# A streaming encoder layer: TensorE, VectorE, ScalarE and GpSimd keep the order of the calls in the first part

## The chip, the cores and the metric

The kernel runs on one core of a Trainium2 chip. The metric is device time in microseconds from launch to end; the median of three runs is given. A core has TensorE (matmuls, PE in the profile, its weight loads PEld), VectorE (DVE), ScalarE (ACT), GpSimd (POOL) and SyncE (SP, which here only issues DMAs). Each engine works through a queue of its own from the front; engines wait for one another, and for DMAs, through semaphores.

## The reference

One layer of a streaming encoder, in float32, over a prompt of 2048 tokens and a sample of 64 tokens, with a model width of 1024. Cut to what matters:

```python
h = rms_norm(x, norm1_g) * (1 + sc1) + sh1            # sc, sh, gt: silu(c) @ w_ada + b_ada, in six parts
glu_a, glu_b, q, k, v, g_conv, g_attn = split(h @ w_in)   # 512 columns each, the gates 1024
u = glu_a * sigmoid(glu_b)
conv_out = silu(layer_norm(causal_depthwise_conv(u, 31 taps) + b_dw)) @ w_conv_out
q, k = rms_norm(q per head), rms_norm(k per head)      # 8 heads of 64
o = band_attention(q, k, v, rel_bias)                  # chunks of 64: own chunk and the 8 before it
x = x + gt1 * ((sigmoid(g_conv) * conv_out + sigmoid(g_attn) * (o @ w_attn_out)) @ w_o)
gate, up = split((rms_norm(x, norm2_g) * (1 + sc2) + sh2) @ w_ffn_in)   # 2816 each
x = x + gt2 * ((silu(gate) * up) @ w_ffn_out)
```

Outputs are the two results, the last convolution inputs, and the keys and values to be cached.

## The kernel before

**Products.** Operands are split into a high and a low part of a shorter format (`hi` by a ScalarE copy, `lo` by a VectorE or GpSimd subtraction), and each product is three matmuls: high by high, high by low, low by high (`mm3`). Weights come by DMA into `wst`, are split into `whi` and `wlo`, stored as split, and loaded again when a later block needs them.

**First part** (it ends at `p1.close()`, line 1689). The 2112 tokens are worked in four blocks (`PBLOCKS`: 576, 512, 512, 512). A block goes through q, a piece of GLU, k, a piece of GLU, v, two pieces of GLU, and the 16 column tiles of the two gates (`ORDER`). Beside these products run, as Python generators:

- the row norm of the next block (`norm_tile`, line 1172): load of `x_t`, squares on ScalarE, the root `r` on GpSimd, the scaled rows on VectorE, transposes `pt` on TensorE, and `h`, `hh`, `hl`;
- the convolution (`convolve`): 31 taps as multiply-adds `y` on VectorE, and its norm (`conv_norm`, line 1289), with sums on GpSimd and a column sum `pm` on TensorE;
- attention (`attend`, line 1495), 8 heads for each block, and 8 for the sample beside block 0: score matmuls `sc`, a maximum and a sum `sm`, exponentials `pr`, transposes `ptp`, the product `po`. The q and k of a head are read back by DMA into `q2` and `kk` (`load_qk`, line 1406); each of the two tiles has one buffer, which in block 0 is divided between a prompt head and a sample head.

**What sets the order.** A planner (`Stream`) adds up a cost for each call and engine, its estimate of the time by which that engine is through. A generator yields the time at which it may go on, and its lane takes it up again when TensorE's estimate has passed that time. For attention this reads:

```python
    def fetch(i):
        if i < len(order) and i not in loaded:
            ...
            loaded[i] = stream.load["pe"] + DMA_LAG
```

`DMA_LAG` is 4000 ns. `attend(i)` calls `fetch(i + 1)` when it has given out its last scores (line 1530), and the next head yields `loaded[i]` (line 1503) before its first score matmul. Two heads may be under way at once.

The sequence of calls that comes of this isn't yet the sequence on the engines. The framework's scheduler takes the calls with their dependencies and sorts each engine's instructions by its own estimate of when they are ready; a call that isn't ready by that estimate lets later ones pass. Edges such as `tc.issue_after(...)`, which the kernel sets in a few places (the first block, the taps behind the last softmax), hold some instructions back.

The relative bias is prepared once, between q and k of block 0 (`bias_rows`, line 1015): a load of `rv` on ScalarE's DMA queue, three VectorE operations that make `rr`, and a store of `rr` to `rb_d` on ScalarE's queue.

**Second part.** Merge, output projection and the feed-forward network, by other pools and lanes. It isn't touched.

Of the kernel before, what the change touches and what calls it, by code (L numbers as in the profile page):

```python
# [589 lines left out]
def weight_order():  # L590
    yield from (("qkv", 0, k) for k in range(4))
    for b, stage in ORDER:
        if stage == "g":
            for g in range(0, 16, 2):
                yield from (("in", 2560 + g * P, h) for h in range(2))
        elif stage in ("q", "k", "v"):
            if b or stage != "q":
                yield from (("qkv", "qkv".index(stage), k) for k in range(4))
        else:
            yield from (("in", CONV + stage * P), ("in", stage * P))  # L600
    for s in range(len(CBLOCKS)):
        for _ in range(2):
            yield from (("ca", c) for c in range(KT))
            yield from (("wo", k) for k in range(KT))
        yield from (("fi", f * P) for f in range(EARLY))
        for f in range(0, NF, 2):
            ops = up_operands(f) + up_operands(f + 1)
            for j in range(0, len(ops), 2):
                yield ("up", *ops[j : j + 2])
                if f >= 2 and seven(s, f - 2):  # L610
                    yield from (("dn", s, f - 2, *DOWN_OPERANDS[i]) for i in {0: (0,), 2: (1, 2), 4: (3,)}.get(j, ()))
                elif j == 0 and f >= 2 and f - 2 not in last_rows(s):
                    yield from (("fo", f - 2), ("fo", f - 1))
        yield from (("fo", f) for f in last_rows(s))
# [3 lines left out]
def streaming_layer(ctx: ExitStack, tc: tile.TileContext, I, O):  # L618
# [159 lines left out]
    def temp(name, shape=(P, 512)):  # L778
        return wk.tile(list(shape), F32, tag="t", name=name, bufs=NT)
# [116 lines left out]
    def mod_steps():  # L896
        for c6, half in MOD_HALVES:
            pa = ps_g.tile([P, 512], F32, tag="gp", name="pa")
            mod_sums(pa[:, : 2 * P], [("mod", c6, half, i) for i in range(4)])
            R = mod_rows(pa[:, : 2 * P])  # L900
            stream.at(
                stream.when("dve") + TURN_LAG, lambda pa=pa, R=R, c6=c6, half=half: mod_columns(pa[:, 2 * P :], R, c6, 4 * half, 2)
            )
            yield
        stream.flush()
        pt = ps_g.tile([P, 512], F32, tag="gp", name="pt")
        pe.transpose(pt[:32, :P], gates_c.rearrange("p c s k -> p (c s k)"), ident)
        row = temp("row")
        dve.tensor_copy(row[:32, :P], pt[:32, :P])
        nc.sync.dma_start(gt_d.rearrange("c s (k n) -> (c s k) n", n=P), row[:32, :P])  # L910
        yield
# [121 lines left out]
    def store_kq(src, n, dst, col, g=None):  # L1033

        pt = ps_g.tile([P, 4, P], F32, tag="gp", name="pt")
        for hp in range(4):
            pe.transpose(pt[:, hp, :n], src[:n, hp * P : (hp + 1) * P], ident[:n, :n])
        stream.after("act", "pe")
        hi, lo = parts(shape=(P, 4, P))
        if g is None:  # L1040
            split(hi[:, :, :n], lo[:, :, :n], pt[:, :, :n])
        else:
            act.activation(hi[:, :, :n], pt[:, :, :n], AF.Copy, scale=g)
            stream.after("dve", "act")
            dve.scalar_tensor_tensor(lo[:, :, :n], pt[:, :, :n], g, hi[:, :, :n].bitcast(F32), ALU.mult, ALU.subtract)

        def store():
            for j, t in enumerate((hi, lo)):
                nc.sync.dma_start(dst[j, :, :, col : col + n].rearrange("h p t -> p h t"), t[:, :, :n].bitcast(F32))

        stream.at(stream.when("act", "dve"), store)

    def store_v(src, n, row):
        vst = wa.tile([P, 4, 4, HD], F32R, tag="x", name="vst", bufs=3)
        s = src[:n].rearrange("p (a c d) -> p a c d", a=4, c=2)
        stream.after("act", "pe")
        act.activation(vst[:n, :, 0:4:3], s, AF.Copy)
        stream.after("dve", "act")
        dve.tensor_tensor(vst[:n, :, 1:3], s, vst[:n, :, 0:4:3].bitcast(F32), ALU.subtract)
        stream.at(stream.when("act", "dve"), lambda: nc.sync.dma_start(  # L1060
            v_d[row : row + n].rearrange("t h d -> t (h d)"), vst[:n].rearrange("p a c d -> p (a c d)").bitcast(F32)
        ))
# [37 lines left out]
    def cached_kv():  # L1100
        rows_ = [(src, j) for j in range(CACHE // P) for src in (ck, cv)]
        ts = []
        for i, (src, j) in enumerate(rows_):
            for src_, j_ in rows_[len(ts) : i + 2]:
                t = temp("cache")
                nc.sync.dma_start(t, src_[j_ * P : (j_ + 1) * P])
                ts.append((t, stream.load["pe"] + CACHE_LAG))
            t, landed = ts[i]
            yield landed
            if src is ck:  # L1110
                store_kq(t, P, k_d, j * P)
            else:
                store_v(t, P, j * P)
            yield
# [506 lines left out]
    xs = first_rows()  # L1621
    W = Weights((nc.sync, act, dve, gps), wpool, dram, stream, list(weight_order()), source, 3, 5, lambda key: key[0] in KEPT)
    first_block(xs)
    norm_lane.add(cached_kv())
    mods = mod_steps()
    norms = {}
# [59 lines left out]
    tail.drain()  # L1686
    stream.flush()
    side.close()
    p1.close()


# [663 lines left out]
```

## Time and profile before

| | |
|---|---|
| runs | 2960.14 us median of 3 (2956.6 to 2961.68) |
| the profiled execution | 2958.2 us |
| its span, first to last instruction | 2956.1 us |
| granted TensorE clock, mean | 0.996 |
| HBM | 476.53 MB read, 148.54 MB written |

Times within the trace are microseconds from the start of the span. In rows of a timeline the columns are start, duration, engine, line, operation, what it writes and reads, shape and count; in brackets stands the idle time of the engine before it and what ended that. Nearly all operations are recorded under line 102, where a helper passes the calls on, so they are told apart by their tiles. A row of the busy times by stage gives the stretch, its length, busy time and number of instructions of each engine, the granted TensorE clock as a share, the share of the DMA engines that was busy, and GB/s.

### The profile page before, as it was taken

What the parts mean: (1) busy time and instruction counts of PE and PEld (TensorE: products, weight loads), DVE (VectorE), ACT (ScalarE), POOL (GpSimd) and SP (SyncE); (2) the same over time, 40 slices, a digit from 0 to 9 for tenths busy, and PEclk for the clock granted to TensorE, in tenths of its full rate; (3) what the DMA queues carried; (4) which work ended last, traced back from release to release, by engine and by line L of the source; (5) the groups of instructions that cost most, each with busy time, mean ns of one, the idle gap of its engine ahead of it and who ended that gap; (6) DMA issues with size and microseconds to landing.
All of it is one profiled execution on the core that took longest, in us unless ns stands there. A gap on an engine that the chain in (4) does not pass through costs nothing.

```text
span 2956.1 us, 44848 instructions
## 1 busy us (share of the span) xinstructions
PE 2895.5 (98%) x16193; PEld 2587.1 (88%) x16193; DVE 2041.9 (69%) x3648; ACT 1363.3 (46%) x2453; POOL 1166.4 (39%) x753
## 2 busy tenths in 40 slices
PE   8999899999999999999999999999999999999999
PEld 5899777787888788888999998999999999999998
DVE  5897687668857885577777746676666547566666
ACT  3345633661465257464433345444444345444442
POOL 1101310111011103454566452366667742465767
PEclk9999999999999999999999999999999999999999
DMA  9988889988987889985444776332333965333333
GB/s 320 320 291 293 285 277 299 286 260 275 303 277 221 277 248 286 280 293 172 150 152 146 261 256 228 99 118 93 114 122 104 332 223 185 97 96 111 115 107 126
DMA packets 467066, 628.04 MB, mean 212 GB/s; under 512 B 36196, under 2 KB 314584, under 8 KB 466845
## 3 DMA queue, kind: packets, MB, share of 16 engines
q1 hardware_dynamic: 452944, 606.11, 63.1%
q10 hardware_dynamic: 13901, 19.08, 1.8%
q8 instruction: 127, 2.08, 0.3%
q14 instruction: 94, 0.77, 0.1%
HBM read 476.53 MB, written 148.54 MB: 211 GB/s over the span
## 4 chain that ended last, share of the span: by engine, by line
PE 48%; DVE 2%; ACT 1%; issue 1%; DMA 0%; POOL 0%; ACTq 0%; DVEq 0%
PE ps L102 29%; PE pd L102 14%; PE pw L102 5%; DVE wlo L102 1%; DVE pw L102 0%; ACT whi L102 0%; DVE ps L102 0%; DVE t L102 0%; DMA tg<-g_d 0%; DVE sums L102 0%; PE pt L102 0%; DVE acc L102 0%; ACT xn L102 0%; DVE hid L102 0%; ACT hid L102 0%
## 5 line engine op out<-in xcount | busy, mean ns | idle before, releaser
L102 PE MATMUL ps<-t,whi 128*128 128x384 f32 (+1 forms) x2112 | 501.7, 322 | 3.0 <-DVE u L102 0.9
L102 POOL TENSOR_TENSOR wlo<-wst,whi 128x1024 fp32r<-128x1024 f32 (+1 forms) x159 | 363.7, 2298 | 243.3 <-ACT whi L102 231.0
L102 ACT ACTIVATE whi<-wst 128x1024 fp32r<-128x1024 f32 (+1 forms) x265 | 258.3, 979 | 321.8 <-PE ps L102 135.0
L102 PE MATMUL ps<-b,whi 128*128 128x384 f32 (+1 forms) x1584 | 381.6, 326 | 6.4 <-ACT early L102 2.7
L102 PEld LDWEIGHTS ps<-t,whi 128*128 128x128 f32 x2112 | 367.7, 188 | 10.2 <-ACT u L102 3.3
L102 DVE SCALAR_TENSOR_TENSOR y<-u,wd,y 128x512 f32<-128x512 f32 (+1 forms) x480 | 369.3, 773 | 6.3
L102 PE MATMUL ps<-hh,whi 128*128 128x512 f32 (+2 forms) x992 | 361.6, 365 | 0.0
L102 DVE TENSOR_TENSOR acc<-acc,pd 128x512 f32<-128x512 f32 x482 | 322.2, 684 | 48.5 <-PE pd L102 46.0
L102 PE MATMUL ps<-hl,whi 128*128 128x512 f32 (+2 forms) x992 | 345.6, 348 | 0.0
L102 PE MATMUL ps<-hh,wlo 128*128 128x512 f32 (+2 forms) x992 | 345.1, 348 | 0.0
L102 PE MATMUL ps<-t,wlo 128*128 128x384 f32 (+1 forms) x1056 | 338.2, 321 | 0.0
L102 PE MATMUL pd<-whi,hid 128*128 128x512 f32 x912 | 297.2, 391 | 0.3 <-DVE hid L102 0.3
L102 PEld LDWEIGHTS ps<-b,whi 128*128 128x128 f32 x1584 | 278.0, 189 | 14.5 <-ACT early L102 4.1
L102 POOL TENSOR_TENSOR r<-t,mhalf 128x1 f32<-128x1 f32 (+2 forms) x68 | 84.1, 1244 | 444.5 <-DVE t L102 434.2
L102 PE MATMUL ps<-b,wlo 128*128 128x384 f32 (+1 forms) x792 | 256.8, 324 | 0.0
L102 ACT ACTIVATE pr<-pr,sm 128x640 f32<-128x640 f32 (+3 forms) x272 | 200.2, 747 | 111.8 <-DVE sm L102 109.2
L102 PEld LDWEIGHTS ps<-hh,wlo 128*128 128x128 f32 x992 | 186.7, 188 | 21.7
L102 PEld LDWEIGHTS ps<-hh,whi 128*128 128x128 f32 x992 | 187.1, 189 | 18.6 <-issue 1.9
L102 DVE TENSOR_TENSOR wlo<-wst,whi 128x1024 fp32r<-128x1024 f32 (+1 forms) x106 | 135.1, 1277 | 98.7 <-ACT whi L102 97.2
L102 PEld LDWEIGHTS pd<-whi,hid 128*128 128x128 f32 x912 | 171.1, 188 | 36.2 <-ACT hid L102 0.7
L102 PEld LDWEIGHTS ps<-hl,whi 128*128 128x128 f32 x992 | 187.5, 189 | 15.5 <-issue 1.4
L102 PEld LDWEIGHTS ps<-t,wlo 128*128 128x128 f32 x1056 | 198.1, 188 | 0.8
(233 smaller groups left out, 6297.4 us busy)
## 6 DMA issues: line engine op xcount, KB each, us to landing
whi<-w_din_h SPq DMA_DIRECT2D x72, 512.0 KB, 6.7
wlo<-w_din_l SPq DMA_DIRECT2D x72, 512.0 KB, 7.5
wst<-sum_d SPq DMA_DIRECT2D x131, 256.0 KB, 2.9
wfo<-in_w_ffn_out SPq DMA_DIRECT2D x64, 512.0 KB, 4.1
wmod<-in_w_ada SPq DMA_DIRECT2D x46, 512.0 KB, 9.0
sum_d<-ws SPq DMA_DIRECT2D x88, 256.0 KB, 2.0
wst<-in_w_ffn_in SPq DMA_DIRECT2D x85, 256.0 KB, 3.3
wst<-in_w_in SPq DMA_DIRECT2D x40, 512.0 KB, 7.6
```

Of the source, the lines that this page charges most:

```text
L102: self.last = f(*args, **kw)
```

## The change

A region is opened after the first block has been set up and closed at the end of the first part. In it, the four named engines get their instructions in the order in which the kernel makes the calls. SyncE isn't among them. No call is added, removed or moved.

```diff
     first_block(xs)
+    ordered = ExitStack()
+    ordered.enter_context(tc.manual_schedule(engines={mybir.EngineType.PE, mybir.EngineType.DVE, mybir.EngineType.Activation, mybir.EngineType.Pool}))
     norm_lane.add(cached_kv())
     mods = mod_steps()
     ...
     side.close()
+    ordered.close()
     p1.close()
```

## The prediction

> **What bounds the kernel now.** I read the page first (busy times), then the busy times by stage, then the waits of TensorE in the first part, then single stretches of the timeline.
>
> ```profile
> span 2956.1 us, 44848 instructions
> PE 2895.5 (98%) x16193; PEld 2587.1 (88%) x16193; DVE 2041.9 (69%) x3648; ACT 1363.3 (46%) x2453; POOL 1166.4 (39%) x753
> ```
> ```profile
> core 0: us, PE busy (x) PEld busy (x) DVE busy (x) ACT busy (x) POOL busy (x), PEclk, DMA share, GB/s
> 62.00:296.00 234.00, 228.42 (x1518) 209.38 (x1517) 192.39 (x339) 108.43 (x221) 39.29 (x37) 1.00 0.88 297
> 296.00:444.00 148.00, 137.94 (x757) 111.97 (x757) 112.99 (x260) 74.01 (x166) 34.16 (x24) 0.97 0.86 282
> 444.00:592.00 148.00, 143.65 (x754) 116.42 (x753) 102.07 (x192) 68.98 (x121) 13.73 (x15) 0.99 0.93 293
> 592.00:1182.00 590.00, 581.68 (x3173) 491.44 (x3173) 438.53 (x843) 298.78 (x543) 74.45 (x62) 1.00 0.83 268
> ```
> ```profile
> engine line waited for: us in total, times, longest us
> PE pt L102 <- DVE x_t L102: 8.2, 3, 5.6
> PE sc L102 <- DVE sm L102: 5.7, 5, 2.4
> PE pm L102 <- POOL s L102: 5.6, 4, 1.9
> PE ps L102 <- DMA whi<-w_dqkv_h: 2.6, 1, 2.6
> PE pt L102 <- DVE kn L102: 1.4, 2, 1.3
> ...
> PE sc L102 <- DMA kk<-k_d: 0.3, 1, 0.3
> ```
>
> TensorE is the bound: 98% over the span. The four stages are what the new region covers after its start; the orders of the two programs differ up to about 1181 us of this trace and are the same behind it. In them TensorE is busy 1091.7 of 1120 us, so all idle time that a better order could win there is 28.3 us. The third fence tells whom TensorE waited for in this stretch. The three largest rows are 19.5 us; waits for the q and k loads of attention are 0.3 us in all. VectorE is at 82, 76, 69 and 74%: second, with room.
>
> **What the order does.** The change adds and removes no computation. In the before kernel a scheduler sorts what the kernel gives out; in the new one each of the four engines keeps the sequence of the calls. Set against each other, 1,480 TensorE instructions have another place, by 7 places on average, and 1,334 on VectorE, 699 on ScalarE, 125 on GpSimd. Since an engine works its queue from the front, an instruction that is moved ahead of its operand holds up all that stands behind it. I therefore looked, on TensorE, for instructions that stand much earlier than before, and asked when the trace shows their operands. SP is not in the region; its loads stay tied to the same events.
>
> **Step A: the first score matmuls of a head.** Tiles `q2` and `kk` have one buffer, so the four loads of the next head can be issued only once the last score matmul of this head is through:
>
> ```profile
> 579.10 0.86 PE L102 MATMUL sc<-kk,q 128*128 128x320 f32 x4
> 583.42 0.39 PE L102 MATMUL ps<-hl,whi 128*128 128x512 f32 x1
> 583.64 0.39 PE L102 MATMUL ps<-hh,wlo 128*128 128x512 f32 x1
> 590.04 0.82 PE L102 MATMUL sc<-kk,q 128*128 128x320 f32 x4 [0.32 <-DMA kk<-k_d]
> ```
> ```profile
> 579.99 0.61 SPq L1418 DMA_DIRECT2D q<-q_d  x1
> 580.65 0.75 SPq L1419 DMA_DIRECT2D kk<-k_d  x1
> 581.45 0.60 SPq L1418 DMA_DIRECT2D q<-q_d  x1
> 582.09 0.79 SPq L1419 DMA_DIRECT2D kk<-k_d  x1
> ```
> ```profile
> kk<-k_d SPq DMA_DIRECT2D x48, 256.0 KB, 6.1
> kk<-k_d SPq DMA_DIRECT2D x16, 80.0 KB, 3.2
> ```
>
> The last score matmul ends at 579.10 + 0.86 = 579.96, and the loads go out from 579.99 to 582.09. The next head's first score matmul came at 590.04 and still waited 0.32 us: the data took 10.1 us from the last score matmul. By the median the last load lands 582.09 - 579.96 + 6.1 = 8.2 us after it. In the scheduler's order 42 to 72 instructions fill such a pause. The kernel's own order gives out the next scores as soon as its estimate says that the load has landed (`DMA_LAG`, 4 us). In blocks 1 to 3, at 11 of the 24 heads, only about seven products of three matmuls lie between: 8 times exactly 21 matmuls, once 21 and a transpose, twice as much work in smaller pieces with 8 transposes. A 128x512 matmul starts 583.64 - 583.42 = 0.22 to 0.23 us after the one before it, so the cover is 21 x 0.227 = 4.8 us. The shortest pauses before, some 42 instructions or 8 us, showed no wait, so the data is usually there within 8; I take 7.3. The wait is 7.3 - 4.8 = 2.5 us, x 11 = **+27 us**. Low end: last issue 2.1 + the shortest median 3.2 = 5.3, so 0.5 x 11 = 6. High end, with 10.1: 58. What hid the load was the transposes and products that now stand behind the scores; they are still done afterwards, so nothing pays for the wait.
>
> **Step B: a block's first head.** In blocks 0 and 1 its first score matmul is moved ahead by 85 and 54 instructions. For block 1:
>
> ```profile
> 457.30 0.44 SPq L1419 DMA_DIRECT2D kk<-k_d  x1
> 468.67 0.74 PE L102 MATMUL sc<-kk,q 128*128 128x320 f32 x4
> ```
>
> Fifty-four places at 0.227 are 12.3 us: TensorE would be there at 456.4, when the last load goes out at 457.30 and lands 6.1 later, at 463.4. That is 7 us if SP stays where it is, 0 if the load moves up as well. For two heads 0 to 14; I take +10, nearer the high end, since the loads stand behind weight loads on SP and the DMA engines are 0.86 to 0.93 busy there.
>
> **Step C: transposes and sums that now stand in front.** In block 1 the first column sum of the convolution's norm stands 25 instructions earlier, yet its operand ended the wait in this row:
>
> ```profile
> 540.39 1.13 PE L102 MATMUL pm<-s,ones 128*128 128x512 f32 x2 [1.27 <-POOL s L102]
> ```
>
> Moved up by 25 x 0.227 = 5.7 us it would wait 1.27 + 5.7 = 7 us. Three groups of `ptp` transposes, moved up likewise, are 3 to 5 us each. Up to 20 in all; most goes away because TensorE comes later there anyway (A and B): **+6**.
>
> **Step D: the bias rows.** The load of `rv` and the store of `rb_d` now stand one behind the other on ScalarE, and VectorE's three `rr` operations between them are late:
>
> ```profile
> L102 DVE TENSOR_SCALAR rr<-rv x1: 281/281/281, 60.0 to 60.0; 8x256 f32<-8x256 f32 x1
> L1018 ACTq DMA_DIRECT2D rv<-in_rel_bias x1: 302/302/302, 17.8 to 17.8; - x1
> ```
> ```profile
> 119.93 1.06 ACT L102 ACTIVATE whi<-wst 128x1024 fp32r<-128x1024 f32 x1 [3.68 <-DMA wst<-in_w_in]
> ```
>
> Before, the load had 42 us. Now ScalarE issues it at about 113 and stands at the store until VectorE has worked down to `rr`, by its queue some 10 us later. Queued behind: a part of the keys, two tanh, and the weight split that ran at 119.93. TensorE waits for that split and for PSUM banks: 0 to 10, **+4**.
>
> **Step E: stalls that go.** The longest wait of the first part:
>
> ```profile
> 341.83 1.09 PE L102 MATMUL pt<-ident,x_t 128*128 128x128 f32 x4 [5.65 <-DVE x_t L102]
> ```
> ```profile
> 323.89 4.62 POOL L102 TENSOR_TENSOR y<-y,s 128x512 f32<-128x512 f32 x4
> 328.48 0.54 POOL L102 TENSOR_TENSOR r<-t,mhalf 128x1 f32<-128x1 f32 x1
> 337.30 1.16 ACT L102 ACTIVATE pr<-pr,sm 128x512 f32<-128x512 f32 x2
> 338.37 0.61 ACT L102 ACTIVATE junk<-x_t 128x512 f32<-128x512 f32 x1
> ```
> ```profile
> 336.00:341.50 5.50, 0.18 (x2) 0.00 (x0) 2.28 (x10) 5.18 (x14) 0.55 (x1) 0.76 1.08 369
> 341.50:348.00 6.50, 6.05 (x25) 4.72 (x26) 6.50 (x18) 4.19 (x8) 2.62 (x1) 0.68 0.73 177
> ```
>
> GpSimd's `r` stood behind four `y` products (4.62 us), ScalarE's squares behind a head's exponentials. In the new order both stand in front. That can end the 8.2 us of `x_t`, and some 2 us lost to the lower clock behind it (6.5 us at 0.68). The other stalls are 5.7, 5.6 and 1.4; the 2.6 us for a weight load stays. I take **-12** (0 to -23); what is late next is the fourth row load itself, then A.
>
> **Step F: the clock after a wait.**
>
> ```profile
> 409.36 0.50 PE L102 MATMUL sc<-kk,q 128*128 128x256 f32 x2 [2.37 <-DVE sm L102]
> 410.50:413.90 3.40, 3.40 (x10) 2.77 (x9) 2.60 (x7) 2.09 (x6) 0.00 (x0) 0.50 1.04 331
> ```
>
> A wait of 2.37 us was followed by 3.4 us at a granted clock of 0.50, which costs 1.7 us. If four of the 13 waits of A and B bring one, that is **+6** (0 to 13 x 1.7 = 22). [...]
>
> **Sum:** 27 + 10 + 6 + 4 - 12 + 6 = +41 us. The profiled execution took 2958.2 us (span 2956.1), 1.9 below the median of the runs, 2960.1. So 2958.2 + 41 + 2 = **3001 us**.
>
> **Rivals.**
> 1. *Faster: the loads come in time.* If the last of a head's loads lands within 4.8 us of its last score matmul, A, B and F vanish, and E decides with C and D small: -12 to -23, **2943 us**. For it: the 3.2 us median of the small loads, and the stalls of E, which the new order does cure. Against it: the 10.1 us of the head shown.
> 2. *The waits are mostly hidden.* Each wait lets VectorE and ScalarE catch up, so later waits go, and A, the low end 6, and B about balance E: +0 to +15, **2968 us**. For it: VectorE at 82% early. Against it: A's waits are for loads, not for an engine.
> 3. *VectorE becomes the bound.* In its new sequence it waits for late scores with the convolution's taps behind. It has 41.6 us of room in the first stage and 151.5 in the last. If each of 40 heads makes it wait 3 to 4 us, convolution and merged norms slip as well: +85, **3045 us**. It decides where VectorE's busy time with waits reaches the length of a stage.
>
> **How the numbers follow.** Forecast 0.55, rival 1 0.14, rival 2 0.15, rival 3 0.16. The forecast's own range is 2975 to 3030 (A from 10 to 45, the rest near its values). The range reaches into rival 1 no further than 2952, and to rival 3: 2952 to 3046. Some 0.2% (6 us) can be told from no change. Rival 1 is faster, 0.14; a third of rival 2 lies within, 0.05; the rest is slower, 0.81.
>
> **What would show it.** Right: among TensorE's waits a row of `sc` for `kk<-k_d` or `q<-q_d` with ten or more entries and 20 us or more (0.3 now), mostly between 490 and 1150 us; the `x_t` row below 3 us; more stretches at clock 0.50. A is wrong if that row stays below 6 us; E if the `x_t` row stays; rival 3 is right if VectorE's waits, not loads, head TensorE's list. The part behind 1182 us should keep its length.

## The result: 100 us slower

The kernel with the region takes 3059.27 us (median of 4 runs, 3052.76 to 3066.94), the kernel before 2959.18 us beside it. The ratio is 1.0339, with a 95% interval of 1.0308 to 1.037. The profiled execution took 3064.4 us, its span is 3062.7 us.

All of the loss lies in the first part. The first matmul of the second part (`ps<-cin`) in the trace of before and in the trace of after (start, duration):

```profile
1186.21 0.56 PE L102 MATMUL ps<-cin,whi 128*128 128x320 f32 x2 [1.40 <-DVE o_p L102]
```
```profile
1292.78 0.56 PE L102 MATMUL ps<-cin,whi 128*128 128x320 f32 x2 [1.40 <-DVE o_p L102]
```

It comes 106.6 us later. From there to the end both take 1769.9 us. The busy times from 62 us to that matmul, first before, then after:

```profile
62.00:1186.10 1124.10, 1094.47 (x6211) 931.20 (x6209) 848.76 (x1635) 551.89 (x1052) 161.63 (x138) 0.99 0.86 279
```
```profile
62.00:1292.70 1230.70, 1127.09 (x6221) 952.30 (x6219) 863.07 (x1641) 549.96 (x1053) 157.14 (x140) 0.97 0.79 256
```

TensorE stands idle for 1230.7 - 1127.1 = 103.6 us instead of 29.6, and is busy for 32.6 us longer with the same matmuls, at a granted clock of 0.97 instead of 0.99. So 74 us more are waits. By an estimate the 33 us are nearly all clock: in these stretches TensorE runs for 78.5 us at clock 0.50 instead of 17.1, and half of the 61.4 us between them, 30.7 us, is the most that this cost. VectorE is busy for 863 of 1230.7 us, 70%: no other engine became the bound. By stage, the same stretches as in the prediction:

```profile
62.00:296.00 234.00, 213.95 (x1381) 193.89 (x1379) 187.70 (x316) 92.92 (x184) 27.62 (x31) 0.98 0.84 284
296.00:444.00 148.00, 123.62 (x663) 104.78 (x664) 84.24 (x207) 71.32 (x163) 35.09 (x26) 0.88 0.70 231
444.00:592.00 148.00, 138.11 (x736) 110.81 (x735) 119.16 (x220) 52.69 (x105) 10.98 (x12) 0.98 0.90 291
592.00:1182.00 590.00, 554.67 (x2952) 462.83 (x2951) 411.67 (x782) 264.70 (x486) 61.46 (x59) 0.98 0.76 247
```

The second stage is the worst: 24 us idle in 148 and a clock of 0.88. Whom TensorE waited for in the first part (us in total, times, longest):

```profile
PE sc L102 <- DMA kk<-k_d: 35.2, 10, 8.8
PE sc L102 <- DVE sm L102: 20.5, 18, 4.8
PE ptp L102 <- ACT pr L102: 20.2, 15, 8.7
PE sc L102 <- DVE h L102: 5.5, 2, 3.2
PE pt L102 <- DVE kn L102: 4.2, 5, 1.3
...
PE sc L102 <- DVE y L102: 2.5, 1, 2.5
PE pt L102 <- DVE x_t L102: 2.1, 2, 1.9
```

The first row was 0.3 us before; it is the wait that steps A and B describe. The next two were 5.7 and 1.4 and aren't waits for loads: the score banks are freed late (`sm` is written right behind the maximum, the VectorE operation that reads the scores), and the probabilities `pr` come late from ScalarE.

**One head's load.** The last score matmul of one head, the last product behind it, and the first score matmul of the next head, in after; then the first and the last of that head's four loads:

```profile
604.79 0.74 PE L102 MATMUL sc<-kk,q 128*128 128x320 f32 x4
...
609.93 0.39 PE L102 MATMUL ps<-hh,wlo 128*128 128x512 f32 x1
614.63 1.41 PE L102 MATMUL sc<-kk,q 128*128 128x320 f32 x4 [4.32 <-DMA kk<-k_d]
```
```profile
605.56 0.61 SPq L1418 DMA_DIRECT2D q<-q_d  x1
...
607.52 0.60 SPq L1419 DMA_DIRECT2D kk<-k_d  x1
```

The loads go out from 605.56, right behind the last score, and the products between end at about 610.3. The data are there at 614.6, 9.1 us after the last score.

**One maximum behind taps.** VectorE and TensorE in after:

```profile
837.50 3.03 DVE L102 SCALAR_TENSOR_TENSOR y<-u,wd,y 128x512 f32<-128x512 f32 x3
840.45 0.67 DVE L102 TENSOR_TENSOR o_p<-other,po 64x512 f32<-64x512 f32 x1
841.04 0.81 DVE L102 CUSTOM_DVE_ANT_0 pr<-sc,bias 128x640 f32<-128x640 f32 x1
```
```profile
836.58 0.74 PE L102 MATMUL sc<-kk,q 128*128 128x320 f32 x4
...
841.91 1.43 PE L102 MATMUL sc<-kk,q 128*128 128x320 f32 x4 [2.06 <-DVE sm L102]
```

The scores are there at 837.3. Their maximum starts at 841.04, behind convolution taps `y` and an `o_p`, and the next score matmul waits 2.06 us for the bank. Taps aren't all: over the 18 waits of this row, the maxima began 50.0 us in all behind their scores, and in that time VectorE spent 19.5 us on taps, 17.8 on other operations, and stood idle for 12.7.

**One softmax behind a store.** The longest wait for `pr`, on ScalarE and on TensorE:

```profile
397.08 0.63 ACT L102 ACTIVATE part_h<-ln 128x512 fp32r<-128x512 f32 x1 [1.39 <-DVE ln L102]
405.50 0.69 ACT L102 ACTIVATE part_h<-pt,gqk 128x512 fp32r<-128x512 f32 x1 [7.79 <-DMA c_d<-part_h]
406.21 0.59 ACT L102 ACTIVATE other<-po 64x512 f32<-64x512 f32 x1
408.71 0.56 ACT L102 ACTIVATE pr<-pr,sm 64x320 f32<-64x320 f32 x1 [1.91 <-DVE sm L102]
```
```profile
409.32 0.58 PE L102 MATMUL ptp<-ident,pr 64*128 64x64 f32 x3 [8.67 <-ACT pr L102]
```

`part_h` has two buffers. ScalarE stands at a split for 7.79 us until a store (`c_d`) has read one of them, and the scaling of `pr` stands behind it in the queue. The longest wait for `sm`, 4.79 us, begins in the same way, on ScalarE; VectorE and TensorE follow:

```profile
325.64 0.26 ACT L102 ACTIVATE part_h<-ln 128x64 fp32r<-128x64 f32 x1 [5.89 <-DMA o_d<-part_h]
327.15 0.16 DVE L102 TENSOR_TENSOR ssq<-ssq 128x1 f32<-128x1 f32 x1 [5.58 <-ACT junk L102]
328.02 1.00 PE L102 MATMUL sc<-kk,q 128*128 128x384 f32 x2 [4.79 <-DVE sm L102]
```

ScalarE waits for a store of `part_h`, its squares (`junk`) come late, VectorE waits for them, and the maximum stands behind that on VectorE. No tap is in it.

### The profile page after: what moved, and what is told of

Its sections match the earlier page's. It is cut to its first block, busy times and chain, and to the rows that moved or that the text cites. A ratio compares the mean times of both kernels' runs of the same rounds, so it can differ in the third digit from the quotient of the medians.

```text
span 3062.7 us, 44860 instructions
## 1 busy us (share of the span) xinstructions
PE 2925.9 (96%) x16193; PEld 2605.7 (85%) x16193; DVE 2057.0 (67%) x3648; ACT 1360.4 (44%) x2453; POOL 1162.9 (38%) x753
## 4 chain that ended last, share of the span: by engine, by line
PE 46%; DVE 2%; ACT 1%; issue 1%; DMA 0%; POOL 0%; ACTq 0%; DVEq 0%; POOLq 0%
PE ps L102 28%; PE pd L102 13%; PE pw L102 4%; DVE wlo L102 1%; ACT whi L102 0%; DVE ps L102 0%; DMA cin<-o_d 0%; DVE pw L102 0%; DVE t L102 0%; DMA tg<-g_d 0%; DVE acc L102 0%; DVE sums L102 0%; PE pt L102 0%; POOL wlo L102 0%; ACT xn L102 0%
## 5 line engine op out<-in xcount | busy, mean ns | idle before, releaser
L102 PE MATMUL ps<-hh,whi 128*128 128x512 f32 (+2 forms) x992 | 369.9, 373 | 0.0
L102 ACT ACTIVATE pr<-pr,sm 128x640 f32<-128x640 f32 (+2 forms) x272 | 198.9, 747 | 279.8 <-DVE sm L102 274.8
L102 PEld LDWEIGHTS ps<-b,whi 128*128 128x128 f32 x1584 | 276.8, 188 | 13.7 <-DVE v L102 3.2
```

The costliest lines, as they stand in the source:

```text
L102: self.last = f(*args, **kw)
```

## The experiments

Except for the change itself and the one whose row gives an interval (7 runs), each kernel was run once, beside the kernel before on the same chip. That kernel took 2958.9 to 2966.3 us there, and the four runs of the change span 14 us, so smaller differences between single runs aren't told apart by the times alone; the waits, and the time at which the second part starts in the traces, tell more. All waits are TensorE's in the first part.

| in order | further edit | us | over before there | `sc` for `kk` | `sc` for `sm` | `ptp` for `pr` |
|---|---|---|---|---|---|---|
| all four (the change) | | 3059.3 | +100 | 35.2 | 20.5 | 20.2 |
| TensorE | | 3021.1 | +55 | 50.9 | 2.5 | 1.6 |
| all but TensorE | | 3045.7 | +79 | 3.7 | 24.6 | 13.7 |
| VectorE | | 3011.4 | +45 | 2.5 | 21.2 | 9.7 |
| ScalarE | | 2990.9 | +25 | 4.2 | 9.6 | 6.2 |
| GpSimd | | 2964.2 | +3 | 0.3 | 6.3 | 1.4 |
| all four | loads 8 us | 3023.5 | +57 | 4.0 | 27.5 | 23.9 |
| all four | bias rows early | 3061.0 | +95 | 38.9 | 20.2 | 19.9 |
| all four | loads 8 us, one tap, 0.3 us | 3174.5 | +208 | 3.6 | 22.9 | 7.8 |
| all four | loads 8 us, two taps, 1.0 us | 3006.0 | +45 | 4.5 | 9.1 | 16.6 |
| all but ScalarE | the same two | 2997.9 | +36 | 4.8 | 7.2 | 9.9 |
| all four | the same two, one ring | 2991.4 | +33 | 3.2 | 9.3 | 9.8 |
| TensorE | loads 8 us | 2972.8 | +7 | 3.3 | 15.1 | 9.1 |
| TensorE | loads 8 us, lag 1.4 us | 2978.9 | +18 | 4.4 | 12.7 | 5.2 |
| TensorE | loads 8 us, two taps, 1.0 us | 2972.5 | +11; ratio 1.0033 (1.0017 to 1.0048) | 5.2 | 15.1 | 2.4 |
| TensorE | the same, one ring | 2972.0 | +13 | 4.4 | 12.4 | 1.8 |

**Whose sequence costs it.** The first theory was that all of it is TensorE's own sequence. (In these diffs the engines' names are shortened.)

```diff
-    tc.manual_schedule(engines={PE, DVE, Activation, Pool})
+    tc.manual_schedule(engines={PE})
```

> The region names TensorE alone; VectorE, ScalarE and GpSimd are sorted by the scheduler as in the kernel before. Theory T (the loss is TensorE's own sequence: score matmuls and transposes placed ahead of their loads and of the softmax, and the half clock behind each such wait): nearly all of the loss stays, 3030 to 3075 us, with the row of sc for kk<-k_d at 25 us or more, ptp for pr at 10 us or more, and ten or more stretches at clock 0.50 in the first part. Rival R (the sequences of the other three engines, above all the convolution's taps standing ahead of the softmax on VectorE, make the operands late): at most 2985 us; the waits for sm, pr and h fall below 10 us together, and only the waits for loads remain.

```diff
+    tc.manual_schedule(engines={DVE, Activation, Pool})
```

> The region names VectorE, ScalarE and GpSimd, but not TensorE, whose instructions are sorted by the scheduler again. Theory T (TensorE's sequence is the loss): 2940 to 2975 us, waits of sc for kk<-k_d below 5 us, at most six stretches at clock 0.50; the x_t stall of the kernel before (8.2 us) may go, as forecast in step E. Rival R (the other engines' sequences are the loss): 3020 us or more, with waits of TensorE for sm, pr, h above 30 us.

TensorE alone in order, then all but TensorE:

```profile
PE sc L102 <- DMA kk<-k_d: 50.9, 13, 7.8
...
PE sc L102 <- DVE sm L102: 2.5, 4, 1.5
...
PE ptp L102 <- ACT pr L102: 1.6, 2, 1.2
```
```profile
PE sc L102 <- DVE sm L102: 24.6, 22, 3.5
PE ptp L102 <- ACT pr L102: 13.7, 15, 2.4
```

Both theories fall as stated; each is half of it. The waits for loads belong to TensorE's sequence. Those for the softmax appear with the other engines' sequences here; that TensorE's own brings some too shows only when the loads' waits are gone (below). Each half alone costs 55 and 79 us, together 100: probably because a wait for the one gives the other time to catch up. The three other engines were then tried one by one.

```diff
+    tc.manual_schedule(engines={DVE})
```

> The region names VectorE alone. Theory T2 (two separate losses: TensorE's sequence waits for the q and k loads, and VectorE's sequence puts convolution taps and splits ahead of the softmax's maximum, which holds the score banks): 3000 to 3045 us, with the row of sc for sm at 15 us or more and the row of sc for kk<-k_d below 4. Rival U (it is ScalarE's sequence: exponentials and scales behind squares, copies and tanh): at most 2985 us, sc for sm below 10.

```diff
+    tc.manual_schedule(engines={Activation})
```

> The region names ScalarE alone. Theory T2: a small part of the loss, 2955 to 2985 us; the row of ptp for pr below 6 us, since ScalarE is at half load and a scale that stands behind a copy waits for less than 1 us. Rival U: 3000 us or more, with ptp for pr at 10 us or more (13.7 where three engines kept their order, 1.6 where only TensorE did).

```diff
+    tc.manual_schedule(engines={Pool})
```

> The region names GpSimd alone. Step E of the prediction has the 8.2 us of waits of pt for x_t end because GpSimd's root r no longer stands behind four products y: by that the row falls below 3 us and the time is 2950 to 2962 us. Rival W (the transposes pt come later in TensorE's own sequence, and that ended the wait; it was 1.3 us where only TensorE kept its order, 6.8 and 9.1 where only ScalarE or only VectorE did): the row stays at 5 us or more, 2960 to 2975 us.

```profile
PE sc L102 <- DVE sm L102: 21.2, 18, 3.5
PE ptp L102 <- ACT pr L102: 9.7, 6, 4.4
PE pt L102 <- DVE x_t L102: 9.1, 1, 9.1
```

These are VectorE's rows: its sequence alone holds the banks as long as the whole change does. ScalarE's costs 25 us, so 6 us more than the 2985 us that were expected at most, spread over several rows of which none is over 10 us. GpSimd's costs nothing that can be told. Its row for `x_t`, and the same where TensorE alone keeps its order:

```profile
PE pt L102 <- DVE x_t L102: 8.8, 3, 6.5
```
```profile
PE pt L102 <- DVE x_t L102: 1.3, 1, 1.3
```

The prediction had GpSimd's order end the `x_t` stall; alone it doesn't. Nor is it shown that TensorE's does: with TensorE alone in order the stalled transposes stand some 7 places earlier than before, and their rows are ready at 341.6 us as before (341.7); TensorE merely comes to them some 6 us later. In the trace of before, the load of the stalled row and its `r` are these:

```profile
328.18 0.96 SPq L1150 DMA_DIRECT2D x_t<-in_x_prompt  x1
340.34 0.55 POOL L102 TENSOR_TENSOR r<-t,mhalf 128x1 f32<-128x1 f32 x1 [11.32 <-DVE t L102]
```

GpSimd had been idle for 11.3 us, so it wasn't late; ScalarE's squares, at 338.37, were.

**The loads.** In `fetch`:

```diff
-            loaded[i] = stream.load["pe"] + DMA_LAG
+            loaded[i] = stream.load["pe"] + 8000.0
```

> The whole region, but the planner takes a head's q and k loads for landed after 8 us of TensorE's work instead of 4. Theory T: the row of sc for kk<-k_d falls from 35.2 us to under 8, and the half-clock stretches that stand behind those waits go too (some 5 to 8 of 16), so 27 to 40 us are won: 3015 to 3035 us; the waits for the softmax (sc for sm 20.5, ptp for pr 20.2) stay as they are. Rival R (VectorE is behind the planner, and the waits for loads only let it catch up): the waits for sm, pr and h grow by about what the loads' waits shrink, 3045 us or more.

```profile
PE sc L102 <- DVE sm L102: 27.5, 26, 3.7
PE ptp L102 <- ACT pr L102: 23.9, 14, 12.0
PE sc L102 <- DMA kk<-k_d: 4.0, 1, 4.0
```

The row falls from 35.2 to 4.0, what is left is block 0's first head, and the number of stretches at half clock behind 62 us from 15 to 8 (from 78.5 to 58.0 us in all). The time falls by 36 us (43 against before). Of the 31 us of waits, 10.7 came back as waits for the softmax. With TensorE alone in order the same edit does nearly all:

> The region names TensorE alone, and the planner takes the q and k loads for landed after 8 us instead of 4. Theory T2: the loads' waits (50.9 us where TensorE alone kept its order) fall below 8, and with them most of the half-clock loss (37.6 us): 2955 to 2985 us. Rival V (a fixed sequence on TensorE loses to the scheduler's by whatever operand is late; take one wait away and the next takes its place): 3000 us or more, waits for sm, pr, h, hl rising by 20 us or more.

From +55 to +7 us. But with the loads' waits gone, the rows of `sm` and `pr` rise from 4.1 to 24.2 us together, though VectorE, ScalarE and GpSimd are sorted by the scheduler here. So part of the softmax's waits comes with TensorE's own sequence, hidden before by the waits for loads. A longer lag for the results of the other engines does no more:

```diff
-PE_LAG = 400.0
+PE_LAG = 1400.0
```

> TensorE alone in order, loads taken for landed after 8 us, and the planner's lag for other engines' results 1400 ns instead of 400 (PE_LAG). Theory T2: what is left of TensorE's waits there (sc for sm 15.1, ptp for pr 9.1) comes from transposes and scores placed too close behind the softmax; it halves, and with it some of the 20.5 us of half clock: 2955 to 2968 us against 2972.8, and 2966.3 before on this chip. Rival V (another operand is late next): 2970 us or more.

The two rows fall from 24.2 to 17.9 us together, but a weight load (5.2) and `pm` (3.5) are late now; it is no faster.

**The bias rows** are given out ahead of the region instead of between q and k of block 0:

```diff
     first_block(xs)
+    bias_rows()
     ordered = ExitStack()
     ...
-            if b == 0 and stage == 1:
-                bias_rows()
```

> The whole region, but the bias rows (load of rv, three VectorE operations, store to rb_d) are given out ahead of it, where the scheduler may place them. By step D of the prediction this is worth 4 us (0 to 10): 3049 to 3059 us, all of it before 180 us of the trace. Rival S (the start of the region, with ScalarE standing at the store and weight splits and PSUM evictions behind it, sets off the later delays, since every queue starts late): 15 us or more, at most 3044 us, and the waits behind 180 us shrink as well.

The time, 3061.0 us, is above both expectations: nothing is won that single runs could tell. The first part ends 3.3 us earlier (1289.5), but TensorE's waits up to 178 us aren't smaller (6.8 us, 5.3 in the change), and those behind stay as they were. The stop of step D does happen in the change: the store goes out at 126.41 us, and the weight split behind it starts at 126.82, 7.07 us after ScalarE's last work. It costs TensorE nothing that these traces show, and the start sets off nothing.

**The taps.** The edits of the convolution's lane, both with the 8 us, all four engines in order:

```diff
-CONV_ROOM = 2000
-    conv, tail = Lane({"dve": CONV_ROOM}, burst=4), Lane({})
+CONV_ROOM = 300       # second version: 1000
+    conv, tail = Lane({"dve": CONV_ROOM}, burst=1), Lane({})     # second version: burst=2
```

> All four engines in order, loads taken for landed after 8 us, and the convolution's lane gives out one tap at a time and only while VectorE's estimate is at most 0.3 us ahead of TensorE's (before: up to four taps, 2.0 us ahead). Theory T2: fewer taps stand ahead of a maximum, the row of sc for sm falls from 27.5 us (8 us loads alone) to 12 or less and the one of ptp for pr (23.9) with it: 2985 to 3008 us against 3023.5. Rival U (ScalarE's sequence): sc for sm and ptp for pr stay above 35 us together, 3012 us or more. It may also go wrong in a third way: the taps come too late, pile up at the end of a block, and the wait moves to pm or to y.

```profile
PE pm L102 <- POOL s L102: 128.7, 9, 33.8
```

It went the third way: the convolution starved and was done at the end of each block, with TensorE waiting at `pm`. I took for each of the 136 maxima the time from the end of its scores to its start, and added up what VectorE spent on taps in that time: 29.5 us before, 65.8 in after, 78.3 with the 8 us, 114.1 with VectorE alone in order, and 1.4 here. Yet the `sm` row is still 22.9 us here, so taps in front aren't the only cause of it. The longest of these waits, on VectorE and on TensorE:

```profile
453.29 0.22 DVE L102 TENSOR_TENSOR part_l<-o_s,part_h 128x64 fp32r<-128x64 f32 x1 [8.69 <-DMA k_d<-part_l]
455.92 1.01 PE L102 MATMUL sc<-kk,q 128*128 128x384 f32 x2 [9.61 <-DVE sm L102]
```

VectorE stands at a split until a store has read `part_l`, with the maximum behind it. The second version:

> All four engines in order, loads taken for landed after 8 us, and the convolution's lane given two taps at a time while VectorE's estimate is at most 1.0 us ahead (2.0 us and four taps in the region as it was; 0.3 us and one tap starved the convolution and cost 128.7 us of waits of pm). Theory T2: VectorE spends less time on taps between the end of a head's scores and the maximum that reads them (78.8 us summed over 136 maxima with 8 us loads alone, 1.4 with the one tap): 50 us or less, the row of sc for sm at 20 us or less, and without a pile at the block's end 3000 to 3018 us. If the taps ahead don't matter: 3020 us or more at the same sc row. If it starves again: a row of pm above 15 us.

```profile
PE ptp L102 <- ACT pr L102: 16.6, 10, 7.2
PE sc L102 <- DVE sm L102: 9.1, 16, 2.0
```

Taps in front of maxima fall to 25.4 us, the `sm` row to 9.1, the time to 3006 us. That fits the taps as a cause of the row, though the run shifts other work as well. The largest row left is ScalarE's `pr`.

**The splits behind stores.** First ScalarE was left out:

```diff
+    tc.manual_schedule(engines={PE, DVE, Pool})
```

> TensorE, VectorE and GpSimd in order, ScalarE sorted by the scheduler, with both cures; against 3006.0 us with ScalarE in order too. If ScalarE's own sequence (exponentials and scales of the softmax behind copies, squares and tanh) makes pr late: the row of ptp for pr falls from 16.6 to 7 us or less, po for ph from 6.2 to 2 or less, and the time is 2975 to 2994 us. If the transposes stand too close behind the softmax in TensorE's sequence: ptp for pr stays at 12 us or more and the time at 2998 us or more.

```profile
PE ptp L102 <- ACT pr L102: 9.9, 4, 7.9
...
PE po L102 <- DVE pl L102: 8.3, 3, 7.8
```

This lies between the two expectations: two single waits of 8 us stand for most of it, and the one for `pr` has ScalarE waiting 7.45 us for a store of `part_h` just ahead. So the buffers were changed, in the same memory, with all four in order and the 8 us and the two taps kept:

```diff
-    NT, NS = 7, 2
+    NT = 11
-            wk.tile(list(shape), F32R, tag="sh", name="part_h", bufs=NS),
-            wk.tile(list(shape), F32R, tag="sl", name="part_l", bufs=NS),
+            wk.tile(list(shape), F32R, tag="t", name="part_h", bufs=NT),
+            wk.tile(list(shape), F32R, tag="t", name="part_l", bufs=NT),
```

> All four engines in order with both cures, as in the 3006.0 us; the two buffers each of part_h and part_l and the seven of the temporaries become one ring of eleven, in the same memory. Theory P (a split that stands in front in ScalarE's and VectorE's sequences waits for a store that still reads its buffer, with the softmax behind it): the row of ptp for pr falls from 16.6 to 10 us or less, po for ph from 6.2 to 2 or less, no wait of part_h for q_d, c_d or o_d over 3 us behind 100 us of the trace, and the time is 2980 to 2996 us. Rival Q (other work of ScalarE, or transposes that stand too close behind the softmax): the two rows stay above 18 us together, 3000 us or more; or the wait moves to the temporaries, which share the ring now.

```profile
PE ptp L102 <- ACT pr L102: 9.8, 10, 2.1
PE sc L102 <- DVE sm L102: 9.3, 17, 1.4
```

The longest wait for `pr` falls from 7.2 to 2.1 us, ScalarE waits for no store of `part_h` any more, and 3006.0 becomes 2991.4 us; in the traces the first part ends 13.0 us earlier (1211.7 us, 1224.7). `po` for `ph` fell only to 4.0 us, where 2 was expected. Two runs asked whether the cures make a version faster than before, with TensorE alone in order:

> TensorE alone in order, with both cures (loads taken for landed after 8 us; two taps at a time and at most 1.0 us ahead). Theory T2: the taps' lane matters less where the scheduler sorts VectorE, so little is won against 2972.8 us (8 us alone): 2958 to 2974 us, no faster than the kernel before by over 0.2%. A version that beats the kernel before would be 2953 us or less. Against it stand the waits that are left there, sc for sm 15.1 and ptp for pr 9.1.

> TensorE alone in order with both cures (2972.5 us, 0.33% slower than before) and the one ring of eleven buffers. Theory P: the waits for pr are 2.4 us there already, since the scheduler lets other ScalarE work pass a split that waits; at most 6 us are won, 2965 to 2974 us. Rival: the ring also ends the waits of sc for sm (15.1 us) by letting ScalarE and VectorE run ahead, 2960 us or less.

They don't: 1.0033 of the time before (1.0017 to 1.0048) and 2972.0 us. No version here was faster than the scheduler's order. With all four engines in order 33 us stay, 8 of them behind the first part, where the first products of the second part wait for VectorE's `t` since the taps' edit; of the rest, the waits for the softmax are single ones of up to 2 us, which I did not follow further.

## Why the prediction was wrong

The direction and the mechanism of the first step held; the time lay above the range, since two steps were sized at 6 us each and measured some 44 and 33.

- **Step A (+27) and B (+10): right.** Nine of the ten waits for `kk` are later heads, 26.4 us, 2.9 each where eleven of 2.5 were forecast; the wait ended 7.1 to 9.1 us behind the last score in eight of them (7.3 was taken). Block 0's first head waited 8.8 us, block 1's nothing. Together 35.2 against 37. The 8 us lag, which takes these waits away, brought 36 us.
- **Step C (+6): the failing step.** The rows of `sm`, `pr`, `kn`, and `sc` for `h` and `y`, rose from 5.7, 1.4, 1.4, 0 and 0 to 20.5, 20.2, 4.2, 5.5 and 2.5, by 44 us. I had looked only at TensorE instructions that moved ahead of operands that stayed where they were, with a cap of 20 us, and held that they would mostly go since TensorE came later there. For that part the reasoning held: with TensorE alone in order the rows of `sm` and `pr` are 4.1 us together, and 24.2 only once the loads' waits are gone. But the operands moved as well: on VectorE taps in front of maxima, on ScalarE and VectorE a softmax behind a split that waits for a store. With TensorE out of the region, the other engines' sequences alone bring 38.3 us in these two rows. How the 44 us divide among taps, stores and other work isn't shown.
- **Step F (+6): failed as well.** I let four of the 13 waits of A and B bring a stretch at half clock of 3.4 us each. Behind 62 us there are 15 stretches instead of 4, and five of them are longer; TensorE's busy time grew by 32.6 us. Five of the 15 stand behind waits for `kk`, about as forecast; the other ten stand behind waits that the sum had at little or nothing, so most of the miss follows from C.
- **Step D (+4): not shown.** ScalarE does stop at the store, as described, but the run with the bias rows early differs by less than the runs of one kernel do.
- **Step E (-12): right in size, wrong in cause.** `x_t` fell by 6.1, `pm` by 4.5, and the weight load's 2.6 went. The `r` shown in the prediction belongs to the row before: the stalled row's own `r` came at 340.34 us, behind ScalarE's late squares. GpSimd's sequence alone left the `x_t` row at 8.8 us, TensorE's alone made it 1.3, with TensorE later and the data no earlier.
- **Rivals.** The third (3045 us) was the nearest in time, and it named VectorE's taps; but VectorE didn't become the bound (70%), and the taps stood ahead of the maxima, not behind. The first is out, since the loads weren't there in 4.8 us; so is the second, since the waits weren't hidden.
- The signs named were met: a `kk` row of 10 entries and 35.2 us, `x_t` at 2.1, more half clock, the same 1769.9 us behind the first part.

## What to carry to other kernels

When several engines get a fixed order, look at each engine's sequence against the operands of all the others: ask of every instruction that another engine waits for (here a maximum that frees a bank, a scaling) what now stands in front of it, and whether that can itself be waiting, for a store's buffer for instance. A planner whose lags are good enough where a scheduler sorts afterwards (4 us, where the data of eight heads came 7.1 to 9.1 us behind the last score) isn't good enough where its order is final. And price the waits of the bound engine with the clock that its trace shows behind them: here 32.6 of the 106.6 us lost were not waits but more busy time of the same matmuls, with 78.5 us at clock 0.50 instead of 17.1.

## What the runs showed of the hardware

**The clock behind waits of TensorE.** In the first part of after, behind 62 us, there are 15 stretches at clock 0.50, 78.5 us in all; before has 4, 17.1 us in all. One of the 15 stands behind the wait of 2.06 us, another begins within the wait of 8.67 us that ended at 409.32 (first row, second row):

```profile
841.90:845.30 3.40, 3.39 (x10) 2.90 (x11) 3.29 (x7) 0.92 (x2) 0.00 (x0) 0.51 0.65 212
405.00:418.60 13.60, 9.28 (x26) 7.44 (x27) 5.17 (x12) 4.26 (x10) 1.64 (x1) 0.50 0.78 252
```

In the second, two 128x512 matmuls that follow one another start 0.43 us apart (411.28 and 411.71); at clock 1.00 it was 0.23 us (609.70 and 609.93). The length of a single wait did not tell here whether such a stretch followed: two waits of 1.08 and 1.09 us, ended at 296.91 and 298.33, had one behind them from 299.2 (3.4 us at 0.50), while behind 3.14 us, ended at 645.66, the clock stayed at 1.00 for the next 6.8 us. What decides it isn't shown.
